# Two-layer hybrid decoder trunk on one core: weight sums in quarter-megabyte pieces, reads moved earlier, stores out of turn, and block attention two rounds deep

## The chip, the cores and the metric

One Trainium2 chip, one of its cores. The metric is the device time of one execution in microseconds (us), the median over several runs. Within a core five engines work beside each other, each on its own list of instructions and in its order: TensorE (PE, matrix products; its weight loads are listed apart as PEld), VectorE (DVE), ScalarE (ACT), GpSimd (POOL) and SyncE (SP, which here only issues DMAs). ACT and POOL issue some DMAs too. An instruction that needs the result of another engine waits at the head of its list, and everything behind it on that engine waits with it.

## The reference, cut to what matters

Two layers over a sequence of 1024 tokens and 1024 channels, float32. One layer:

```python
h = _rms_norm(x, pre_g)
proj = jnp.einsum('bsd,dc->bsc', h, w_in)
sb_qkv, ssm_u, ret_qkv, lru_u, gates, merge = jnp.split(proj, SPLITS, axis=-1)
...
mix = jnp.stack([y_sb, y_ssm, y_ret, y_lru], axis=2).astype(dtype)
mix = mix * jax.nn.silu(gates.reshape(bsz, s, N_BRANCH, BRANCH_WIDTH))
y = jnp.einsum('bsnw,nwd->bsnd', mix, w_branch)
gate = jax.nn.sigmoid(merge.reshape(bsz, s, N_BRANCH, D_MODEL))
merged = jnp.sum(gate * y, axis=2)
out = jnp.einsum('bsd,de->bse', merged, w_out)
return x + _rms_norm(out, post_g)
```

The four mixers are a stick-breaking attention (4 heads of 64, in query blocks of 128), an S5 state space model that ends in GELU and a gated linear unit (GLU), a retention in chunks of 128, and an RG-LRU. The projection `w_in` has 3072 columns for the mixers and their gates (256 for each) and 4096 for the merge gates.

## The kernel before, in words

**Tiling.** Each layer is done in two halves of the sequence, c = 0 and c = 1, of 512 tokens. All large products are of 128x128 weights with 128x512 data in fp32r; float32 accuracy comes from three products (`mm3`, L1200) of a high part `wh` and a low part `wl` of each weight tile with a high and a low part of the data. The gate columns of both halves are multiplied together in a Strassen-like scheme: products of sums of the input (`xs_t`, and the on-chip pieces that hold them, `tab`) with sums of four weight blocks, whose partial results v1, u2, u3 and gate results go to DRAM (`v`, `u`, `ge`) and are fetched back later (`fetch`, L1226).

**The order of the work** is written by hand: the scheduler does not reorder anything. `plan_layer` (L160) lists the fillers of a layer: projections `p` of half 0 with groups `x` of Strassen products between them, projections of half 1, groups `y`, the output product `o` of half 0, groups `z` and merge products `m` of half 1, its output product. Each filler is made of *half fillers*: one weight tile of 128x512 (256 KB), twelve matmuls. There are 268 half fillers in a layer; the number of one is its *position* (p of half 0 and x: 0 to 71, p of half 1: 72 to 103, y: 104 to 179, o: 180 to 195, z and m: 196 to 251, o: 252 to 267).

**What stands ahead of each half filler** is `half(s)` (L1679): `ahead(s)` (L225), where SP issues the reads of weight tiles up to s+9 (`raw`, 8 buffers) and tile s+3 is split (`split`, L111: ACT copies `wh` from `raw`, DVE subtracts to `wl`); `put_late()` (L363), by which SP issues the stores that were asked for at least two positions ago; one function of the list `hooks`; and `planned(l, p)` (L1608), which takes the side generators one step on at the positions that the table `PLAN` gives them: `prep` (parameters, on POOL), `tb` (input of half 1), `lru0/1`, `s50/51` (S5), `ret0/1`, `sb0/1` (attention), `post0/1` (residual and output), `sum` (`wsums`).

**What the change touches.** `wsums(l)` (L1631) makes the sums of the gate weights from DRAM to DRAM: ACT issues copies (`ws<-in_wq_dram`), and POOL issues DMAs that add to them (L1634), each over one piece of 128x2560 floats, 1280 KB. `summed` marks a sum as issued; a weight tile that is a sum (`raw<-ws`) is read after it. `prologue_t(c)` (L392) normalises a half of the input; its squares are made by ACT and added up by POOL (L404). `sba(l, c)` (L1068) is the attention: for each of 16 rounds (4 query blocks by 4 heads) scores on PE against the stored keys `kS` (L106), sigmoids on ACT, a scan and subtraction on DVE (L94), in the next round the transposes of the weights on PE (L1108), and after each second head the product with the values. The queries of a block are read back by SP from DRAM (L1083, `g<-q`); `project` stores them there. `fetch_y` (L1243) fetches what a mixer kept; `gated` (L1232) then multiplies on DVE. `prefetch` (L1270) asks for v1 or u3 one filler ahead, `filler` fetches u2 at its own start. `post` (L1181) adds the residual, which `load_res` reads. `macc` adds merge results on POOL (L1256). All scratch tiles of 128x512 on chip (`G`) come from one pool of NGEN = 50.

```python
# sba, L1078
def queries(b):
    put_late(0)
    S["q", c, b] = (G(F32R), G(F32R))
    for k in range(2):
        assert stored[id(qmem[c][b][k])] == l
        sp.dma_start(S["q", c, b][k].bitcast(F32), qmem[c][b][k])
```

Of the kernel before, what the change touches and what calls it, by code (L numbers as in the profile page):

```python
# [40 lines left out]
def hybrid_kernel(ctx: ExitStack, tc: tile.TileContext, x, xt, ws, wq, wb, par, bcw, preg, postg, con, rot, out, dbg=None):  # L41
# [183 lines left out]
    def ahead(s):  # L225
        load_to(s + NRAW + 1)
        split_to(s + 3)
# [164 lines left out]
    def prologue_t(c):  # L392
        gc = S["par", 0][:, C_PG:C_PG + 8]
        hc = H(F32)
        xk = hc
        for k in range(KD):
            sp.dma_start(xk[k], xt[k, :, c * T:(c + 1) * T])
        yield 0
        acc = G()
        actv(acc, xk[0], AF.Square)  # L400
        for k in range(1, KD):
            sq = G()
            actv(sq, xk[k], AF.Square)
# [12 lines left out]
        yield 0  # L416
        yield from build(hc)
# [650 lines left out]
    def sba(l, c):  # L1068
# [8 lines left out]

        def queries(b):  # L1078
            put_late(0)
            S["q", c, b] = (G(F32R), G(F32R))  # L1080
            for k in range(2):
                assert stored[id(qmem[c][b][k])] == l
                sp.dma_start(S["q", c, b][k].bitcast(F32), qmem[c][b][k])  # L1083

        queries(0)
        for i in range(n + 3):
            yield 3
            if i % 4 == 1 and i < n - 4:
                queries(i // 4 + 1)
            if i >= 2 and i - 2 < n and js[i - 2][1] % 2:  # L1090

                pair = [J.pop(i - 3), J.pop(i - 2)]
# [88 lines left out]
    def post(u):  # L1181
        load_res(u, range(2))
        yield 0
        out_stat(0, NT)
        for t in range(NT):
            yield 0
            out_put(u, t, False)
            load_res(u, range(t + 2, min(t + 3, NT)))
# [37 lines left out]
    def fetch(src, u):  # L1226
        assert stored[id(src)] == u
        t = G()
        sp.dma_start(t, src)
        return t  # L1230
# [12 lines left out]
    def fetch_y(u, n):  # L1243
        l, c = units[u]
        drain(("lru", "s5", "ret", "sb")[n] + str(c))
        put_late(0)
        for j in range(2):
            S["yf", n, j] = fetch(yd[c][n][j], l)
# [20 lines left out]

    def prefetch(l, i):  # L1270

        c, kind, *a = plans[l][i + 1]
        if kind == "y":
            S["v1", a[0]] = fetch(v1d[a[0]], l)
        elif kind == "z":
            for q in a:
                S["u3", q] = fetch(u3d[q], l)

    def filler(l, i, half):
# [66 lines left out]
        elif kind == "z":  # L1346
            m = len(a)
            ps = [A() for _ in range(m)]
            for k in range(2 * m):
                half(s + k)  # L1350
                q, odd = a[k % m], k < m
                if k == 0:
                    for r in a:
                        S["u2", r] = fetch(u2d[r], l)
                        if r % 5 == 0:
                            fetch_y(u, r // 5)
# [21 lines left out]
    def project(u, i, s, half):  # L1378
# [41 lines left out]
        elif i in (9, 11):  # L1420
# [21 lines left out]
            def rest():  # L1442
                for _, _, r_, rd, _ in todo:
                    copy(rd, r_.bitcast(F32))
                if pq:
                    for b in range(NT):
                        for k, t in enumerate(S.pop(("q", b))):
                            store(qmem[c][b][k], t[:, :].bitcast(F32))

            hooks.append(rest)  # L1450
# [180 lines left out]
    def wsums(l):  # L1631
# [3 lines left out]

        for n in ORDER0[l]:
# [22 lines left out]
    with tc.manual_schedule():  # L1659
        dve.memset(ones1, 1.0)  # L1660
        warm = const.tile([P, T], BF16, name="warm")
# [40 lines left out]
NGEN = 50  # L1702
# [13 lines left out]
        "sum": (40, 46, 53, 60, 66, 72, 79, 86, 92, 98, 105, 112, 118, 124, 131, 138, 144, 150, 157, 164, 170),  # L1716
        "sb0": (42, 43, 45, 46, 48, 49, 51, 52, 54, 55, 57, 58, 60, 61, 63, 64, 66, 67, 69, 70, 72, 73, 75, 76, 78, 79, 81, 82, 84, 85, 87, 88, 90, 91, 93, 94, 96, 97, 99, 100),
# [7 lines left out]
    },  # L1725
# [6 lines left out]
        "sum": (30, 37, 44, 51, 58, 65, 72, 79, 86, 93, 100, 107, 114, 121, 128, 135, 142, 149, 156, 163, 170),  # L1732
# [6 lines left out]
    },  # L1739
# [122 lines left out]
```

## Time and profile before

| what | before |
|---|---|
| median of the timed runs (two: 2109.9 and 2103.89) | 2106.89 us |
| the profiled execution, its own time | 2102.62 us |
| its span in the profile | 2100.8 us |
| mean granted clock of TensorE | 0.931 |
| PE busy | 1811.7 us |
| DVE, ACT, POOL busy | 1354.3, 914.5, 408.9 us |
| moved by DMA | 439.52 MB in 213757 packets |

The profile is of one execution. Busy times say how long an engine worked; PE's is the largest. A wait of PE is listed with the engine and line (or the DMA) that ended it. The granted clock is TensorE's: 1.00 is its upper level (2.4 GHz), 0.50 its lower one (1.2 GHz). Line numbers are those of the kernel before.

### The profile page before, as it was taken

The numbers are of one execution on the slowest core, as the hardware profiler recorded it, in microseconds if no ns is written. First come the engines' busy times: TensorE is split into PE (matmuls) and PEld (weight loads), VectorE is DVE, ScalarE is ACT, GpSimd is POOL, SyncE is SP. The second block draws the span as 40 slices with busy tenths as digits, with TensorE's granted clock in tenths as the row PEclk, the third lists the DMA queues.
The fourth block names the chain that finished last, engine by engine and source line by source line (L and its number), as shares of the span: only waits on it lengthen the run. The fifth ranks groups of instructions, "written<-read, shape, count | busy, mean of one in ns | idle before, by whom it ended". The sixth has DMA issues, their size and how long they took to land. (4 is left out here: it accounts for less than half of the span.)

```text
span 2100.8 us, 26957 instructions
## 1 busy us (share of the span) xinstructions
PE 1811.7 (86%) x8730; PEld 1469.7 (70%) x8730; DVE 1354.3 (64%) x2400; ACT 914.5 (44%) x1817; POOL 408.9 (19%) x704
## 2 busy tenths in 40 slices
PE   9576989886997999797899977988799999988997
PEld 6455767764876777676777756767577877766776
DVE  7485466854676774764647875558567767656675
ACT  5465435552332344333455644435433334443333
POOL 6943000000021220586600000000000212100231
PEclk9788999998998999899999988999799999998999
DMA  5259687468888946544526597882889987554543
GB/s 175 84 182 352 203 263 242 126 202 282 231 280 262 296 141 209 195 136 134 163 80 212 182 329 247 262 267 81 239 277 286 299 269 239 179 202 144 169 142 105
DMA packets 213757, 439.52 MB, mean 209 GB/s; under 512 B 25585, under 2 KB 34161, under 8 KB 212593
## 3 DMA queue, kind: packets, MB, share of 16 engines
q1 hardware_dynamic: 203376, 353.92, 49.6%
q0 software_dynamic: 8704, 41.95, 10.6%
q10 hardware_dynamic: 1536, 41.95, 5.4%
q8 instruction: 69, 1.13, 0.2%
q14 instruction: 72, 0.58, 0.1%
HBM read 340.59 MB, written 180.36 MB: 248 GB/s over the span
## 5 line engine op out<-in xcount | busy, mean ns | idle before, releaser
L1207 PE MATMUL pa<-g,wh 128*128 128x512 f32 x2816 | 923.7, 408 | 84.1 <-DVE g L94 46.4
L1207 PEld LDWEIGHTS pa<-g,wh 128*128 128x128 f32 x2816 | 543.3, 197 | 210.1 <-issue 49.0
L94 DVE TENSOR_TENSOR wl<-raw,wh 128x512 fp32r<-128x512 f32 x536 | 408.4, 767 | 347.1 <-ACT wh L91 345.5
L1207 PE MATMUL pa<-g,wl 128*128 128x512 f32 x1368 | 551.1, 403 | 9.2 <-DVE wl L94 9.1
L91 ACT ACTIVATE wh<-raw 128x512 fp32r<-128x512 f32 x536 | 325.3, 626 | 132.5 <-PE pa L1207 64.2
L94 DVE TENSOR_TENSOR g<-g,g 128x512 f32<-128x512 f32 (+7 forms) x427 | 303.6, 719 | 79.8 <-ACT g L91 28.8
L88 ACT ACTIVATE g<-g 128x512 f32<-128x512 f32 (+1 forms) x212 | 132.0, 629 | 488.3 <-DVE g L94 475.1
L1207 PEld LDWEIGHTS pa<-g,wl 128*128 128x128 f32 x1368 | 268.5, 196 | 70.6 <-DVE wl L94 12.0
L94 DVE TENSOR_TENSOR g<-pa,g 128x512 f32<-128x512 f32 x227 | 156.4, 690 | 188.6 <-PE pa L1207 102.5
L1256 POOL TENSOR_TENSOR g<-g,g 128x512 f32<-128x512 f32 x96 | 139.8, 1492 | 512.1 <-DVE g L94 504.3
L1207 PE MATMUL pa<-tab,wh 128*128 128x512 f32 x560 | 187.0, 403 | 12.8 <-DMA tab<-xs_t 12.8
L91 ACT ACTIVATE g<-g 128x512 fp32r<-128x512 f32 (+2 forms) x208 | 112.0, 547 | 173.5 <-DVE g L103 56.2
L1634 POOL DMA_DIRECT2D ws<-in_wq_dram x16 | 14.6, 912 | 698.9 <-DMA ws<-in_wq_dram 698.9
L1207 PE MATMUL pa<-wh,g 128*128 128x512 f32 x448 | 142.2, 399 | 7.3 <-DVE g L94 6.0
L91 ACT ACTIVATE g<-pa 64x128 fp32r<-64x128 f32 (+3 forms) x190 | 92.5, 487 | 109.1 <-PE pa L1207 96.6
L91 ACT ACTIVATE g<-pb 128x128 f32<-128x128 f32 (+5 forms) x227 | 85.5, 421 | 120.2 <-PE pb L106 61.4
L1207 PEld LDWEIGHTS pa<-tab,wh 128*128 128x128 f32 x560 | 107.8, 195 | 36.8 <-DMA tab<-xs_t 11.9
L1207 PE MATMUL pa<-tab,wl 128*128 128x512 f32 x320 | 127.2, 397 | 0.0
L106 PE MATMUL pb<-kS,g 128*128 128x512 f32 (+2 forms) x192 | 57.8, 401 | 57.7 <-DMA g<-q 32.4
L1207 PEld LDWEIGHTS pa<-wh,g 128*128 128x128 f32 x448 | 85.2, 193 | 26.9 <-DVE g L94 6.8
L88 ACT ACTIVATE g<-pb 128x512 f32<-128x512 f32 (+4 forms) x203 | 87.1, 511 | 37.5 <-PE pb L106 22.3
L1207 PE MATMUL pb<-wh,g 128*128 128x512 f32 x320 | 99.3, 392 | 1.0 <-DVE g L94 1.0
(172 smaller groups left out, 1937.1 us busy)
## 6 DMA issues: line engine op xcount, KB each, us to landing
raw<-in_ws_dram SPq DMA_DIRECT2D x192, 256.0 KB, 3.6
ws<-in_wq_dram ACTq DMA_DIRECT2D x32, 1280.0 KB, 9.3
raw<-ws SPq DMA_DIRECT2D x160, 256.0 KB, 4.2
raw<-in_wq_dram SPq DMA_DIRECT2D x120, 256.0 KB, 5.0
ws<-in_wq_dram POOLq DMA_DIRECT2D x16, 1280.0 KB, 11.9
ws<-ws POOLq DMA_DIRECT2D x16, 1280.0 KB, 12.1
u<-g SPq DMA_DIRECT2D x80, 256.0 KB, 5.5
g<-u SPq DMA_DIRECT2D x80, 256.0 KB, 3.5
```

The costliest lines, as they stand in the source:

```text
L88: act.activation(out, in_, func, **kw)
L91: act.activation(out, in_, AF.Copy, **kw)
L94: dve.tensor_tensor(out, a, b, op=op)
L106: pe.matmul(out, lhsT=lhsT, rhs=rhs, start=start, stop=stop)
L1207: pe.matmul(ps, lhsT=a, rhs=b, start=start and i == 0, stop=stop and i == 2, skip_group_check=more)
L1256: pool.tensor_tensor(acc, acc, sg, op=ALU.add)
L1634: pool.dma_start(a, b, accum_op=ALU.add, max_dma_last_dim=5120)
```

## The change

- **Sums by quad.** `wsums` makes each sum in five pieces of 128x512, as the weight tiles are read, each piece with its own copies and additions; ACT issues 160 copies instead of 32 and POOL 160 additions instead of 32. The steps in `PLAN["sum"]` go from 21 to 50 a layer, over positions 38 to 168 (40 to 170 and 30 to 170 before). The old function stays in the file, unused.
- **Reads.** `ahead` asks SP for weight tiles up to s+8 instead of s+9; `split_to` is the same. `prefetch` looks up to four fillers ahead: v1 and u3 up to five half fillers, u2 up to three, and u2 is no longer fetched at the filler's own start. `post` reads one residual piece at a time, ahead of each output step.
- **Stores out of turn.** `stored_now(o)` issues one store early, when something is about to read it; `fetch` and `queries` call it, and `put_late(0)`, which issued all pending stores there, is gone.
- **Query copies** (ACT) and their stores are spread over four hooks, one for each block, instead of one.
- **Attention.** `dp = 2 - c`: in half 0 the transposes of a round come two rounds after its scores instead of one, in half 1 one as before. The queries of the first block are read at position 34 instead of 42 (layer 0), 40 instead of 48 (layer 1) and 106 instead of 116 (half 1); those of the next blocks one round earlier.
- **Input of half 1.** The squares are added up by DVE (`tt`) instead of POOL, seven additions of 128x512.
- **Tables.** The steps of S5 are moved (`s51`: the last ones at 91, 92, 93, 95, 97, 99, 100 instead of 93 to 99; `s50` of layer 0 stretched to 86). The pool has 51 tiles, with the warm-up tile now in it.

```diff
     def ahead(s):
-        load_to(s + NRAW + 1)
+        load_to(s + NRAW)
         split_to(s + 3)
...
+    def stored_now(o):
+
+        for k, e in enumerate(late):
+            if e[0] is o:
+                sp.dma_start(o, e[1])
+                stored[id(o)] = e[3]
+                late.pop(k)
+                return
...
             actv(sq, xk[k], AF.Square)
-            pool.tensor_tensor(acc, acc, sq, op=ALU.add)
+            tt(acc, acc, sq, ALU.add)
...
+        dp = 2 - c
         def queries(b):
-            put_late(0)
             S["q", c, b] = (G(F32R), G(F32R))
             for k in range(2):
+                stored_now(qmem[c][b][k])
...
-        for i in range(n + 3):
+        for i in range(n + dp + 2):
             yield 3
-            if i % 4 == 1 and i < n - 4:
+            if i % 4 == 0 and i < n - 4:
                 queries(i // 4 + 1)
...
-            if 1 <= i <= n:
-                st = J[i - 1]
+            if dp <= i < n + dp:
+                st = J[i - dp]
...
     def prefetch(l, i):
...
+        for k in range(i + 1, min(i + 5, len(plans[l]))):
+            c, kind, *a = plans[l][k]
+            for name, d, reach in (("v1", v1d, 5),) if kind == "y" else (("u3", u3d, 5), ("u2", u2d, 3)) if kind == "z" else ():
+                for q in a if k == i + 1 or base[l, k] - base[l, i] <= reach else ():
+                    if (name, q) not in asked[l]:
+                        asked[l].add((name, q))
+                        S[name, q] = fetch(d[q], l)
...
+            for b in range(NT):
+                hooks.append(lambda b=b: rest(b))
...
+        def cols(a, j):
+            return a[:, 512 * j:512 * j + 512]
+
+        for n in ORDER0[l]:
+            s1, s2, s3, s4 = (wsum[l][j][n] for j in range(4))
+            for j in range(6):
+                if j < 5:
+                    act.dma_start(cols(s3, j), cols(wq[l, n, 2], j))
+                    act.dma_start(cols(s2, j), cols(wq[l, n, 3], j))
+                if j:
+                    add(cols(s3, j - 1), cols(wq[l, n, 0], j - 1))
+                yield 0
+                if j:
+                    add(cols(s2, j - 1), cols(s3, j - 1))
+            summed.update(((l, 1, n), (l, 2, n)))
...
-NGEN = 50
+NGEN = 51
```

**SP, the first query read of layer 0, half 0** (`raw`: weight tiles; `xs`, `xs_t`, `v`: stores of input sums and of Strassen results; `q_0_0`: the queries of block 0). Before, at position 42:

```order
L212 DMA raw_2036<-in_wq_dram 128x512
L366 DMA xs_t_2_304<-g_1983 128x512
L366 DMA xs_t_6_308<-g_1817 128x512
L366 DMA xs_t_2_320<-g_1986 128x512
L366 DMA xs_t_6_324<-g_1919 128x512
L366 DMA xs_t_3_297<-g_2062 128x512
L366 DMA xs_t_7_301<-g_2009 128x512
L1083 DMA g_2071<-q_0_0_262 128x512
L1083 DMA g_2072<-q_0_1_263 128x512
L212 DMA raw_2087<-in_wq_dram 128x512
```

After, at position 34 (L1093 is L1083 of before):

```order
L212 DMA raw_1772<-in_ws_dram 128x512
L366 DMA v_4_150<-g_1710 128x512
L1093 DMA g_1787<-q_0_0_262 128x512
L1093 DMA g_1788<-q_0_1_263 128x512
L212 DMA raw_1805<-in_ws_dram 128x512
L366 DMA v_10_156<-g_1739 128x512
L366 DMA xs_1_287<-g_1755 128x512
```

The read stands eight half fillers earlier, and the six stores that were issued with it at once are no longer ahead of it.

**PE, the second round of that attention** (`kS_94`, `kS_95`: keys of the second and third head; `pa` rows: matmuls of half fillers). Before, with the transpose of the first round (L1108) ahead of the second round's scores:

```order
L1207 MATMUL pa_2129<-g_674,wl_2039 128x512
L1108 MATMUL pb_2220<-cons,g_2104 128x128
L106 MATMUL pb_2224<-kS_94,g_2071 128x256
L106 MATMUL pb_2224<-kS_94,g_2072 128x256
L106 MATMUL pb_2224<-trib,identb 128x128
L1207 MATMUL pa_2130<-g_671,wh_2089 128x512
```

After, the second round:

```order
L1217 MATMUL pa_2137<-g_672,wl_2010 128x512
L106 MATMUL pb_2190<-kS_94,g_1787 128x256
L106 MATMUL pb_2190<-kS_94,g_1788 128x256
L106 MATMUL pb_2190<-trib,identb 128x128
L1217 MATMUL pa_2138<-g_669,wh_2045 128x512
```

And after, the third round (L1118 is L1108 of before; L985 belongs to the retention):

```order
L1217 MATMUL pa_2137<-g_680,wl_2143 128x512
L985 MATMUL pb_2289<-cons,g_1966 128x128 x4
L1118 MATMUL pb_2296<-cons,g_2083 128x128
L106 MATMUL pb_2300<-kS_95,g_1787 128x256
L106 MATMUL pb_2300<-kS_95,g_1788 128x256
L106 MATMUL pb_2300<-trib,identb 128x128
```

The transpose of the first round's weights has moved behind the half fillers between the second and the third round; nothing of the rounds is left out.

**POOL, the sums of layer 0 beside the end of `prep` (L505, L738) and the retention's memsets (L984).** Before:

```order
L738 COPY gp_2049<-gp_893 64x8x16
L984 MEMSET g_2380 128x512
L984 MEMSET g_2381 128x512
L1634 DMA ws_1_0_118<-ws_2_0_122 256x1280
L505 TENSOR_TENSOR gp_893<-cons,par_343 32x128
L505 TENSOR_TENSOR g_2407<-g_2407,gp_893 32x4x32
L505 TENSOR_TENSOR gp_893<-cons,par_343 32x128
L505 TENSOR_TENSOR g_2408<-g_2408,gp_893 32x4x32
L1634 DMA ws_2_2_124<-in_wq_dram 256x1280
```

After (L1646, L747, L993 are L1634, L738, L984 of before):

```order
L1646 DMA ws_1_0_118<-ws_2_0_122 128x512
L1646 DMA ws_2_0_122<-in_wq_dram 128x512
L747 COPY gp_2056<-g_698 64x8x16
L747 COPY gp_2056<-gp_891 64x8x16
L747 COPY gp_2056<-g_698 64x8x16
L747 COPY gp_2056<-gp_891 64x8x16
L1646 DMA ws_1_0_118<-ws_2_0_122 128x512
L1646 DMA ws_2_0_122<-in_wq_dram 128x512
L993 MEMSET g_2392 128x512
L993 MEMSET g_2393 128x512
L1646 DMA ws_1_0_118<-ws_2_0_122 128x512
```

There are more additions, each of a fifth of the bytes, and they stand between POOL's other work, also ahead of the copies and memsets that stood ahead of the sums' second step before.

## Rows read from the trace of the kernel before

**Rows 1.** The page, busy time of each engine.

```profile
PE 1811.7 (86%) x8730; PEld 1469.7 (70%) x8730; DVE 1354.3 (64%) x2400; ACT 914.5 (44%) x1817; POOL 408.9 (19%) x704
```

**Rows 2.** Waits of PE, whole run: us in total, times, longest.

```profile
PE pa L1207 <- DVE g L94: 52.3, 16, 7.5
PE pb L106 <- ACT g L91: 43.8, 13, 11.3
PE pb L1108 <- DVE g L94: 37.5, 16, 6.4
PE pb L106 <- DMA g<-q: 32.4, 4, 18.0
PE pb L106 <- POOL g L404: 21.4, 1, 21.4
```

**Rows 3.** Windows: us, PE, PEld, DVE, ACT, POOL busy, clock, DMA share, GB/s.

```profile
69.70:88.90 19.20, 0.00 (x0) 0.00 (x0) 5.24 (x6) 5.20 (x9) 18.26 (x29) 0.50 0.14 41
91.00:97.00 6.00, 6.00 (x15) 4.65 (x16) 3.47 (x16) 3.36 (x5) 5.05 (x25) 0.50 0.00 0
100.00:106.00 6.00, 6.00 (x28) 4.98 (x27) 5.33 (x17) 3.67 (x10) 5.26 (x19) 1.00 0.00 0
140.00:230.00 90.00, 67.66 (x293) 54.91 (x292) 53.24 (x83) 47.61 (x91) 19.26 (x38) 0.87 1.02 339
178.00:725.00 547.00, 459.73 (x2382) 374.15 (x2380) 345.69 (x634) 211.75 (x418) 57.52 (x74) 0.93 0.79 244
```

**Rows 4.** Groups of instructions, DVE's and POOL's additions: busy, mean ns, idle before.

```profile
L94 DVE TENSOR_TENSOR g<-g,g 128x512 f32<-128x512 f32 (+7 forms) x427 | 303.6, 719 | 79.8 <-ACT g L91 28.8 <-DMA g<-y 27.7 <-ACT g L88 11.2
...
L404 POOL TENSOR_TENSOR g<-g,g 128x512 f32<-128x512 f32 x7 | 9.6, 1372 | 0.4
```

**Rows 5.** Source line of the first query reads, 150 to 200 us.

```profile
L1083 SPq DMA_DIRECT2D g<-q x2: 582/605/628, 194.8 to 195.4; - x2
```

**Rows 6.** Waits of PE by stretch: 262:430, then 1300:1530 (two), 430:512 (two), 825:1000.

```profile
PE pb L1108 <- DVE g L94: 15.4, 6, 6.4
...
PE pb L1108 <- DVE g L94: 15.8, 7, 4.5
PE pb L106 <- ACT g L91: 12.1, 3, 6.1
...
PE pa L1207 <- DMA tab<-xs_t: 12.3, 4, 8.0
PE pb L106 <- ACT g L91: 6.1, 1, 6.1
...
PE pa L1207 <- DVE g L94: 27.1, 7, 7.5
```

**Rows 7.** DMA issues, 628 to 652 us (two), and in the whole run: KB, us to landing.

```profile
ws<-ws POOLq DMA_DIRECT2D x1, 1280.0 KB, 19.2
...
g<-y SPq DMA_DIRECT2D x2, 256.0 KB, 17.2
...
g<-y SPq DMA_DIRECT2D x32, 256.0 KB, 4.5
```

**Rows 8.** Waits of SP, 950 to 975 us.

```profile
SPq L1229 <- POOL g L1256: 18.3, 1, 18.3
```

**Rows 9.** The page, DMA queues: packets, MB, share of 16 engines.

```profile
q1 hardware_dynamic: 203376, 353.92, 49.6%
q0 software_dynamic: 8704, 41.95, 10.6%
q10 hardware_dynamic: 1536, 41.95, 5.4%
```

**Rows 10.** Source lines of the sums: a copy's issue (ACT), an addition's issue (POOL).

```profile
L1638 ACTq DMA_DIRECT2D ws<-in_wq_dram x8: 496/496/604, 178.3 to 1478.5; - x8
...
L1634 POOL DMA_DIRECT2D ws<-in_wq_dram x16: 879/884/1166, 200.3 to 1741.4; - x16
```

More of the change, by code (lines that the diff above doesn't have):

```diff
@@ L1085, in sba @@
         queries(0)
-        for i in range(n + 3):
+        for i in range(n + dp + 2):
             yield 3
-            if i % 4 == 1 and i < n - 4:
+            if i % 4 == 0 and i < n - 4:
                 queries(i // 4 + 1)
-            if i >= 2 and i - 2 < n and js[i - 2][1] % 2:
-                pair = [J.pop(i - 3), J.pop(i - 2)]
+            if 0 <= i - dp - 1 < n and js[i - dp - 1][1] % 2:
+                pair = [J.pop(i - dp - 2), J.pop(i - dp - 1)]
                 b, pq = pair[0]["b"], pair[0]["h"] // 2
@@ L1181, in post @@
     def post(u):
-        load_res(u, range(2))
+        load_res(u, range(1))
         yield 0
@@ L1186, in post @@
             yield 0
+            load_res(u, range(t + 1, min(t + 2, NT)))
             out_put(u, t, False)
-            load_res(u, range(t + 2, min(t + 3, NT)))
     def load_res(u, ts_):
@@ L1226, in fetch @@
     def fetch(src, u):
+        stored_now(src)
         assert stored[id(src)] == u
@@ L1245, in fetch_y @@
         drain(("lru", "s5", "ret", "sb")[n] + str(c))
-        put_late(0)
         for j in range(2):
@@ L1268, in pair @@
             macc(u, n, 2 * i + e, odd if e else S.pop(("ge", 5 * n + 1 + i)), py)
+    asked = [set() for _ in range(DEPTH)]
     def prefetch(l, i):
[L1272 to L1277, printed above, removed]
+        for k in range(i + 1, min(i + 5, len(plans[l]))):
[5 more added lines that the diff above has]
+                        S[name, q] = fetch(d[q], l)
     def filler(l, i, half):
@@ L1353, in filler @@
                     for r in a:
-                        S["u2", r] = fetch(u2d[r], l)
                         if r % 5 == 0:
@@ L1440, in project, with rest @@
                 stt(r_, z, 0.125, q_.bitcast(F32), ALU.mult, ALU.subtract)
-            def rest():
-                for _, _, r_, rd, _ in todo:
+            def rest(b):
+                for _, _, r_, rd, _ in todo[2 * b:2 * b + 2]:
                     copy(rd, r_.bitcast(F32))
                 if pq:
[L1446 to L1450, printed above, removed]
+                    for k, t in enumerate(S.pop(("q", b))):
+                        store(qmem[c][b][k], t[:, :].bitcast(F32))
+            for b in range(NT):
+                hooks.append(lambda b=b: rest(b))
         elif i < 8:
@@ L1634, in add, with wsums_old @@
             pool.dma_start(a, b, accum_op=ALU.add, max_dma_last_dim=5120)
+        def cols(a, j):
[12 more added lines that the diff above has]
+            summed.update(((l, 1, n), (l, 2, n)))
+        for n in range(4):
+            s1, s2, s3, s4 = (wsum[l][j][n] for j in range(4))
+            for j in range(6):
+                if j < 5:
+                    act.dma_start(cols(s1, j), cols(wq[l, n, 2], j))
+                    act.dma_start(cols(s4, j), cols(wq[l, n, 1], j))
+                if j:
+                    add(cols(s1, j - 1), cols(wq[l, n, 3], j - 1))
+                    add(cols(s4, j - 1), cols(s2, j - 1))
+                yield 0
+            summed.update(((l, 0, n), (l, 3, n)))
+    def wsums_old(l):
+        def add(a, b):
+            pool.dma_start(a, b, accum_op=ALU.add, max_dma_last_dim=5120)
         for n in ORDER0[l]:
@@ L1660, in hybrid_kernel @@
         dve.memset(ones1, 1.0)
-        warm = const.tile([P, T], BF16, name="warm")
+        warm = G(BF16)
         dve.memset(warm, 0.0)
@@ L1712 @@
         "lru0": (12, 13, 14, 15, 17, 19, 21, 23, 24, 25, 26),
[1 row of a table removed]
[1 row of a table added]
         "ret0": (46, 48, 51, 53, 55, 58, 60, 62, 65, 67, 69, 72, 74),
         "tb": (14, 15, 16, 17, 19, 20, 21, 22, 23, 24, 26, 27, 28, 29, 30, 31, 33, 34, 35, 36, 37, 38, 40, 41, 42, 43, 44, 45, 47, 48, 49, 50),
-        "sum": (40, 46, 53, 60, 66, 72, 79, 86, 92, 98, 105, 112, 118, 124, 131, 138, 144, 150, 157, 164, 170),
-        "sb0": (42, 43, 45, 46, 48, 49, 51, 52, 54, 55, 57, 58, 60, 61, 63, 64, 66, 67, 69, 70, 72, 73, 75, 76, 78, 79, 81, 82, 84, 85, 87, 88, 90, 91, 93, 94, 96, 97, 99, 100),
[1 row of a table added]
         "pro": (246, 248, 250, 252, 254, 256, 257, 259, 261, 263, 265, 267),
@@ L1720 @@
         "lru1": (78, 80, 82, 83, 85, 87, 89, 91, 92, 94, 96),
[1 row of a table removed]
[1 row of a table added]
         "ret1": (104, 106, 108, 110, 111, 113, 115, 117, 119, 120, 122, 124, 126),
[1 row of a table removed]
[1 row of a table added]
         "post0": (197, 199, 200, 202, 203, 205),
+        "sum": (38, 41, 43, 46, 48, 51, 53, 56, 58, 61, 63, 66, 68, 71, 73, 76, 78, 81, 83, 86, 88, 91, 93, 96, 98, 101, 104, 106, 109, 112, 115, 118, 120, 123, 126, 129, 132, 134, 137, 140, 143, 146, 148, 151, 154, 157, 160, 162, 165, 168),
     },
@@ L1728 @@
         "lru0": (8, 9, 10, 12, 13, 14, 17, 21, 23, 25, 27),
[1 row of a table removed]
[1 row of a table added]
         "ret0": (56, 58, 60, 62, 64, 66, 68, 70, 72, 74, 76, 78, 80),
         "tb": (9, 10, 12, 13, 15, 16, 18, 19, 21, 22, 24, 25, 27, 28, 30, 31, 32, 34, 35, 37, 38, 40, 41, 43, 44, 46, 47, 49, 50, 52, 53, 55, 56),
-        "sum": (30, 37, 44, 51, 58, 65, 72, 79, 86, 93, 100, 107, 114, 121, 128, 135, 142, 149, 156, 163, 170),
[1 row of a table removed]
[1 row of a table added]
         "lru1": (78, 80, 82, 83, 85, 87, 89, 91, 92, 94, 96),
[1 row of a table removed]
[1 row of a table added]
         "ret1": (104, 106, 108, 110, 111, 113, 115, 117, 119, 120, 122, 124, 126),
[1 row of a table removed]
[1 row of a table added]
         "post0": (197, 199, 200, 202, 203, 205),
+        "sum": (38, 41, 43, 46, 48, 51, 53, 56, 58, 61, 63, 66, 68, 71, 73, 76, 78, 81, 83, 86, 88, 91, 93, 96, 98, 101, 104, 106, 109, 112, 115, 118, 120, 123, 126, 129, 132, 134, 137, 140, 143, 146, 148, 151, 154, 157, 160, 162, 165, 168),
     },
```

15 rows, old and new, of the table PLAN are left out of this document.

## Prediction

> **What bounds the kernel now.** I read the busy times first. PE works 1811.7 us of the 2100.8 us span [rows 1], more than any other engine, and the order lists the same matmuls after the change as before; so what can be won is PE's idle time, 289 us, and the time at the lower clock. DVE, at 64%, is second and matters stretch by stretch. Then the waits of PE [rows 2]: no single one rules. Matmuls of half fillers wait for DVE additions 52.3 us in 16 waits, scores for ACT 43.8, transposes (L1108) for DVE's weights 37.5 in 16, scores for the query reads (g<-q) 32.4 in only 4, and one wait for POOL's squares (L404) is 21.4. Then windows [rows 3], which show where these stand: from 140 to 230 us the DMA share is 1.02, so transfers are the bound there, while over 178 to 725 us (half 0 of layer 0, with the sums in it) it is 0.79 and DVE is busy 346 of 547 us. Last, the clock: in the 19.2 us without a matmul it stands at 0.50 and stays there just after it, where 6.0 us hold 15 matmuls, against 28 in 6.0 us at 1.00 [rows 3]. A mean of 0.931 over the span means that 0.069/0.5, 13.8% or 290 us, lie at the lower level. About half of that will be idle time itself; the other half, some 145 us of work, would take 72 less. Per microsecond of idle time that is 72/289 = 0.25. Most waits that go here are short, so I give 0.15 us of clock for each.
>
> **What goes, part by part.** A half filler is twelve matmuls; at 28 in 6.0 us it takes 2.6 us.
>
> (a) Squares on DVE. POOL is busy 18.3 of the 19.2 us in which PE stands, yet its seven additions cost 9.6 us [rows 3, 4]; the rest is parameter work ahead of them in POOL's list. On DVE seven additions cost 7 x 0.719 = 5.0 us [rows 4], beside ACT's squares, and DVE is busy 5.2 of those 19.2 us, so there is room. About 2 us of the wait should stay: 19.4 saved. Bounds: all 21.4 saved, or, if DVE's 5.0 us only push its next work back, 16.4.
>
> (b) Query reads. The 18.0 us wait ends on a read that SP issued at 194.8 us and that landed 4.7 us later [rows 5]: SP was late, not the read slow. In the new order the first read stands eight half fillers earlier, 8 x 2.6 = 21 us of PE work, and six stores no longer stand right ahead of it. That would cover 18.0 if SP were as late as before. But the stretch has a DMA share of 1.02 [rows 3], its bytes are the same, and what is not waited for here may be waited for at the next weight tile. Bounds 0 and 32.4; I take 20 of the 32.4. `load_to` one tile less far ahead moves SP's other DMAs of a half filler forward and no byte; its buffers come free at the same splits: nothing.
>
> (c) Attention two rounds deep. The transposes wait 15.4 us for DVE in half 0 of layer 0 and 15.8 in that of layer 1, 31.2 of the 37.5, the longest 6.4 [rows 2, 6]. The transpose moves one round later, two or three half fillers or 5 to 8 us, behind work that does not need it. So nearly each of these waits is covered: 30. Bounds 0 (if DVE is behind by as much a round later) and 31.2.
>
> (d) Sums in small pieces. At 628 to 652 us the fetch of a mixer's output (g<-y) takes 17.2 us, against 4.5 in the middle over the run, with pieces of 1280 KB in flight [rows 7]; DVE waits 27.7 us for g<-y in all [rows 4], and the longest ACT wait of PE, 11.3, stands behind one of these [rows 2]. Input sums read into tab cost 12.3 in 430 to 512 us [rows 6]. With 256 KB pieces the fetch should be near 4.5, 12.7 less, and the 11.3 go; of the tab waits I take 4.7, since those reads are many. 16 of 23.6; bounds 0 and 23.6.
>
> By the Trainium skill, page "DMA: Bandwidth & Descriptors", section "Queues, rings and completion order", a DMA engine takes its queues in turn, a packet at a time. A big piece then holds up SP's queue by at most a packet and piece size matters less than packet size; here the packets of both kinds shrink, so by it all 23.6 would go, and the sum would be 7.6 better. The 17.2 against 4.5 shows that something holds reads up, but not which of the two.
>
> (e) S5's last steps. PE waits 12.1 in layer 1 and 6.1 in layer 0 for ACT ahead of the GLU [rows 6]; its steps are now spread. I take 12 of 18.2, less 5 for tab reads that these waits hide: 7. Bounds 0 and 18.2.
>
> (f) z fetches. Of the waits for DVE at 825 to 1000 us, 27.1 in 7 [rows 6], some come from operands that arrive late: SP stood 18.3 us there behind POOL's merge addition [rows 8]. Asking up to three half fillers, 7.8 us, earlier for u2 and going past pending stores helps part of it; the rest is DVE's own work. 8; bounds 0 and 27.1.
>
> Idle time gone: 19.4 + 20 + 30 + 16 + 7 + 8 = 100.4. With 0.15 x 100 = 15 for the clock, 115.
>
> **What is added.** ACT issues 128 more copies of 0.496 us each [rows 10], 63.5 us in all over two layers. ACT is busy 212 of 547 us there [rows 3], so most of it lies in idle time; behind such an issue stand the splits and the attention's sigmoids, for which PE waits. Bounds 0 and 63.5; a tenth and a little, 7. POOL issues 128 more additions of 0.884 us, 113 us, and is busy 57.5 of 547 [rows 3, 10]; but an addition that waits for its copy holds up the end of `prep` and the retention's memsets behind it, for which ACT, DVE and SP wait. The waits are shorter than before, since a piece is a fifth. Bounds 0 and 113; I take 5. Spread hooks, the 51st tile, the residual reads: nothing; the next half filler's twelve matmuls hide a 0.5 us copy, and without that cover each would cost its 0.5 us.
>
> Last, what is late next. With PE ahead, the same DVE work (346 of 547 us), splits and reads are asked for sooner. I give back a fifth of 115, 23. Net: 115 - 12 - 23 = 80. The profiled execution took 2102.62 us, its span and 1.8 around it, 4.3 under the median of 2106.89. 2102.6 - 80 = 2023.
>
> **The rivals.**
>
> R1, slower: additions priced by the packet. The POOL queue q0 has 8704 packets in 10.6% of 16 engines' span [rows 9]: 0.106 x 2100.8 x 16 / 8704 = 0.409 us each. These are 272 packets to each of the 32 additions. 160 additions of 128 rows and as many closing packets in the same proportion (144) make 23040. At 0.409 us they take 589 us of the sixteen engines instead of 223, 183 more a layer; 178 to 725 us has 0.79 x 547 = 432 us taken, 615 is 68 over its length. Twice 68 is 136; the gains that don't hang on DMA, (a) and (c) less costs, 38, leave 2200. It decides where the spare 115 us a layer are used up, at 315 ns a packet. Against it: q10 takes 1.18 us for a packet of 27 KB and q1 82 ns for one of 1.74 KB [rows 9]: these two go by bytes, at 23 and 21 KB a us, so for an addition's packet of 2 KB, where one of 4.8 KB takes 409 ns, I expect about half of that.
>
> By the Trainium skill, the same page, section "Anatomy of one DMA", a DMA issued by GpSimd costs about 2.0 us fixed and its bytes at 436 KB a us: an estimate of 2.6 us for 256 KB and 5.0 for 1280 KB, thus 416 us for 160 instead of 160 for 32. That speaks for R1. The trace has 19.2 us for one 1280 KB addition from issue to landing [rows 7], so what it waits for or shares outweighs a fixed 2.0 there.
>
> R2, transfers stay the bound: the bytes of 140 to 230 us are what they were, and waits of (b) and (d) only change their names. 64.4 of idle time and 10 of clock, less 12 and a fifth of 74, 15: 47 saved, 2055. For it: the share of 1.02. Against it: single reads waited 18.0 though they landed in 4.7.
>
> R3, nothing is given back: (a) to (e) go whole, 21.4 + 32.4 + 31.2 + 23.6 + 18.2 = 126.8, and the clock's 19 pay for the added issues and more: 1975. For it: DVE is idle over a third of the time. Against it: the 5 us waits follow DVE's chain itself.
>
> R4, DVE is behind: the transposes of (c) wait as long a round later. 70.4 and 10.6 of clock, less 12 and 16: 53, 2050. For it: the 52.3 us of plain DVE waits. Against it: 346 of 547.
>
> **How the numbers follow.** My forecast .47, R3 .17, R2 .15, R4 .13, R1 .08. 2023 is the likeliest. The range reaches down to R3 with a margin and up past R2 and R4: 1970 to 2075; R1 and a little beside it stay out. A measurement here can tell about 2%, 42 us, from no change, so faster means under 2065 (under 2061 against the profiled execution). The forecast gives .43 faster and .04 same, R3 .17 faster, R2 and R4 (10 and 15 us under that bound) together .165 faster and .115 same, R1 .07 slower and .01 same: .765, .165, .07, rounded below.
>
> **What would show it.** Right: no wait of PE on POOL's squares; g<-q waits under 13 us in all; L1118 waits (the former L1108) under 8 us, all but a few in half 1; g<-y landing near 4.5 us beside the sums; PE's mean clock about 0.95; PE idle about 190 us. A q0 share under 13% of the engines' time is against R1, over 25% for it. Wrong: DMA share at 1.0 through 178 to 725 us; SP or ACT waiting on POOL in layer 0's `prep`; new waits on wh or wl, by which ACT's added issues would cost more than 7 us; a DVE wait in place of each transpose wait.

## The result, and the profile after

The changed kernel took 2032.92 us (two runs, 2029.35 and 2036.49) against 2106.89 before: 74 us less, ratio 0.9649, 95% interval 0.9555 to 0.9743. The forecast was 2023, 80 us less.

The page of the changed kernel, busy times and DMA queues, answers to [rows 1] and [rows 9]:

```profile
PE 1808.2 (89%) x8730; PEld 1464.3 (72%) x8730; DVE 1355.4 (67%) x2407; ACT 917.7 (45%) x1819; POOL 522.2 (26%) x825
...
q1 hardware_dynamic: 203376, 353.92, 51.2%
q0 software_dynamic: 23040, 41.95, 13.1%
q10 hardware_dynamic: 23040, 41.95, 6.0%
```

The span is 2027.6 us, 73.2 less. PE is busy 3.5 us less and idle 219.4 us instead of 289.1, so nearly all of it is idle time. The additions' queue has the 23040 packets that were counted beforehand, at 0.131 x 2027.6 x 16 / 23040 = 184 ns each: well under the 315 ns from which rival R1 would have decided. Its share, 13.1%, is just above the 13% that the forecast named as a sign against R1, and far from the 25% for it.

PE's waits in the changed kernel, whole run (us in total, times, longest), answer to [rows 2]:

```profile
PE pa L1217 <- DVE g L94: 39.2, 15, 7.0
PE pa L1217 <- DMA tab<-xs_t: 23.7, 6, 7.2
PE pb L106 <- DMA g<-ubuf: 22.9, 3, 11.3
PE pb L106 <- ACT g L91: 20.4, 12, 3.9
PE pb L106 <- DVE g L94: 20.3, 11, 4.8
PE pa L1217 <- ACT g L91: 19.3, 4, 7.2
PE pb L1118 <- DVE g L94: 17.3, 9, 3.7
```

The wait for POOL's squares and those for g<-q are gone from the list. The waits for ACT ahead of `pb` matmuls went from 43.8 to 20.4, those of half fillers for DVE from 52.3 to 39.2. Two have grown: reads of S5's input (g<-ubuf) from 1.9 to 22.9, and of Strassen's input sums (tab) from 12.8 to 23.7.

The transposes' total hides two changes. Half 0, now two rounds deep, has none of these waits left. Half 1, one round deep in both kernels, has new ones. First the kernel before from 430 to 1030 us (half 1 of layer 0; in that of layer 1 it has none), then the changed kernel from 430 to 1022 and from 1500 to 2030 us:

```profile
PE pb L1108 <- DVE g L94: 1.9, 1, 1.9
...
PE pb L1118 <- DVE g L94: 8.8, 5, 3.7
...
PE pb L1118 <- DVE g L94: 8.5, 4, 3.6
```

So 35.6 us went in half 0 and 15.4 came up in half 1. The change also moved nearly all steps of half 1's attention (`sb1`) two to four positions forward, and its first ten; no run undoes the former.

The fetches of mixer outputs (g<-y) beside the sums did not come near 4.5 us. Issues of the changed kernel from 585 to 600 us (the place of the 17.2 us of [rows 7]), then from 640 to 656 us:

```profile
g<-y SPq DMA_DIRECT2D x2, 256.0 KB, 6.9
...
g<-y SPq DMA_DIRECT2D x2, 256.0 KB, 14.4
```

The first was 17.2 before; the second is of the next mixer, whose two fetches took 2.9 and 4.5 before. The middle of the eight fetches of that part is 8.1 us, 7.1 before. What did fall is DVE's waits for them, from 27.7 to 6.0 us, none of which is for the 14.4.

One of the forecast's signs of being wrong came up: SP waits for POOL in layer 0's `prep`. POOL's waits from 190 to 222 us, then SP's from 205 to 222 us (L771 copies a table of `prep` for S5; L514 is an addition of `prep`):

```profile
POOL ws L1646 <- DMA ws<-in_wq_dram: 18.4, 3, 7.5
...
SPq L771 <- POOL g L514: 7.1, 1, 7.1
```

POOL stands 18.4 us ahead of additions whose sources have not landed yet, and `prep` stands behind them in its list. Before, SP has no wait for POOL there.

Windows of the changed kernel (us, PE, PEld, DVE, ACT, POOL busy, clock, DMA share, GB/s), answer to the last two of [rows 3]:

```profile
140.00:230.00 90.00, 81.46 (x455) 65.52 (x454) 58.70 (x99) 48.95 (x98) 35.84 (x52) 0.96 1.02 329
178.00:725.00 547.00, 483.89 (x2532) 395.29 (x2532) 368.59 (x665) 228.28 (x450) 117.51 (x134) 0.95 0.85 248
```

From 140 to 230 us PE works 81 us instead of 68, at the same DMA share of 1.02: the transfers are still full there, and PE stands less beside them (the changed kernel is some 20 us further on in its work by then).

Where the gain comes up can be read by the weight tiles: the end of ACT's split number n (`wh<-raw`, counted from 0), of which there are 268 in a layer, set against the changed kernel's (us; worked out from the traces of single executions, whose own spread is some 10 us; the last row is the end of the span).

| n | changed | before | one deep | old S5 steps | paced | later |
|---|---|---|---|---|---|---|
| 32 | 127.7 | +15.8 | -0.7 | -0.5 | +0.2 | -0.7 |
| 64 | 253.5 | +22.8 | -1.5 | -1.8 | -9.9 | -19.6 |
| 128 | 534.7 | +36.7 | +20.2 | +15.5 | -6.3 | -27.8 |
| 160 | 638.1 | +50.8 | +20.2 | +15.5 | -6.3 | -27.5 |
| 256 | 981.8 | +53.7 | +20.5 | +22.5 | -6.3 | -20.0 |
| 400 | 1556.9 | +74.2 | +28.1 | +39.0 | -12.0 | -56.9 |
| 536 | 2027.6 | +73.2 | +22.1 | +34.6 | -18.6 | -51.2 |

Before, 37 of the 73 us were lost by n = 128, 14 more between 128 and 160, and 20 in half 0 of layer 1. The other columns are experiments below.

### The profile page after: what moved, and what is told of

Same layout as the page of the kernel before. It is cut to its first block, busy times and chain, and to the rows that moved or that the text cites. A ratio compares the mean times of both kernels' runs of the same rounds, so it can differ in the third digit from the quotient of the medians.

```text
span 2027.6 us, 27353 instructions
## 1 busy us (share of the span) xinstructions
PE 1808.2 (89%) x8730; PEld 1464.3 (72%) x8730; DVE 1355.4 (67%) x2407; ACT 917.7 (45%) x1819; POOL 522.2 (26%) x825
## 3 DMA queue, kind: packets, MB, share of 16 engines
q1 hardware_dynamic: 203376, 353.92, 51.2%
q0 software_dynamic: 23040, 41.95, 13.1%
q10 hardware_dynamic: 23040, 41.95, 6.0%
## 5 line engine op out<-in xcount | busy, mean ns | idle before, releaser
L1217 PE MATMUL pa<-g,wh 128*128 128x512 f32 x2816 | 918.3, 405 | 65.3 <-DVE g L94 30.6
L94 DVE TENSOR_TENSOR wl<-raw,wh 128x512 fp32r<-128x512 f32 x536 | 404.3, 760 | 351.4 <-ACT wh L91 332.5
L94 DVE TENSOR_TENSOR g<-g,g 128x512 f32<-128x512 f32 (+7 forms) x434 | 313.1, 730 | 41.6 <-ACT g L91 16.1
L1646 POOL DMA_DIRECT2D ws<-in_wq_dram x80 | 72.0, 900 | 629.4 <-DMA ws<-in_wq_dram 596.3
L1217 PE MATMUL pa<-tab,wh 128*128 128x512 f32 x560 | 190.3, 409 | 23.7 <-DMA tab<-xs_t 23.7
L1646 POOL DMA_DIRECT2D ws<-ws x80 | 70.0, 875 | 265.1 <-DMA ws<-in_wq_dram 186.3
L88 ACT ACTIVATE g<-pb 128x512 f32<-128x512 f32 (+4 forms) x203 | 87.2, 511 | 31.2 <-PE pb L106 19.4
```

The lines of the kernel that those rows point to most:

```text
L88: act.activation(out, in_, func, **kw)
L94: dve.tensor_tensor(out, a, b, op=op)
L1217: pe.matmul(ps, lhsT=a, rhs=b, start=start and i == 0, stop=stop and i == 2, skip_group_check=more)
L1646: pool.dma_start(a, b, accum_op=ALU.add, max_dma_last_dim=5120)
```

## The experiments

All are built on the changed kernel. Its own time is 2033 (2032.92, and 2034.45 in a second series of four runs, 2028.92 to 2038.43). The other medians are of four runs, which lie 2 to 20 us apart, so a difference under some 6 us is not told apart.

**The same kernel again.** No edit.

> The changed kernel once more, as the measure for the others of this series on the same chip. Every theory: 2033 us, within 5.

2034.45, ratio to before 0.9635 (0.9596 to 0.9675).

**Squares on POOL.**

```diff
-            tt(acc, acc, sq, ALU.add)
+            pool.tensor_tensor(acc, acc, sq, op=ALU.add)
```

> The changed kernel with the seven additions of squares of half 1's input on POOL again. By the forecast: the wait of PE at about 67 us comes back with some 20 us, +22 with the clock: about 2055 us. By the rival that what follows (the build of half 1's input on DVE, 12.9 us of wait before, 7.2 now) decides when that stretch ends: +10 us or less, or, if the stretch gets longer by DVE's late start too, +27.

2047.33, ratio 0.9709 (0.9676 to 0.9742): 13 us slower. The waits of PE from 60 to 135 us, squares on POOL:

```profile
PE pb L106 <- POOL g L413: 21.5, 1, 21.5
PE pa L1217 <- ACT g L91: 9.5, 1, 9.5
```

The wait is back whole, and the next one, for half 1's input, is 9.5 where the changed kernel has 7.2 and the kernel before 12.9. Of these some 20 us, 13 reach the end. The forecast's mechanism holds, its size less a third.

**Attention one round deep.**

```diff
-        dp = 2 - c
+        dp = 1
```

with the old steps of `sb0` after the first.

> The changed kernel with the attention of half 0 one round deep again (transposes a round after the scores, the old steps), the first queries still read early. By the forecast: the transposes wait some 30 us more in half 0, +35 with the clock, less a fifth, +28: about 2061 us. By the rival that DVE is behind anyway and two rounds only move the wait: under +10 us.

2051.79, ratio 0.9727 (0.9692 to 0.9763): 18 us slower. First line of PE's waits, whole run, one round deep:

```profile
PE pb L1118 <- DVE g L94: 64.2, 26, 12.6
```

The transposes wait 47 us more than in the changed kernel, all of it in half 0. Yet only 18 us come out at the end: in the table the loss begins between n = 64 and 128, is 20 in layer 0 and hardly grows in layer 1. The rival's "under 10" falls; the forecast's 28 was too much. Other waits are shorter here: g<-ubuf fell from 22.9 to 12.2.

**First queries late.**

```diff
-        "sb0": (34, 42, 43, 45,
...
+        "sb0": (42, 42, 43, 45,
...
-        "sb1": (106, 116, 119,
...
+        "sb1": (116, 116, 119,
...
```

(and 40 to 48 in layer 1).

> The changed kernel with the first queries of each half read at the old positions (42, 48, 116). By the forecast most of (b) hangs on the lead of eight half fillers: PE waits for g<-q again, some 15 to 20 us over the run, +15 to +20 us: about 2050. By the rival that SP's order (no pending stores ahead of the read, tiles a half filler less ahead) did it: g<-q waits under 8 us and under +6 us.

2031.71, ratio 0.9616 (0.9578 to 0.9655): no change that can be told. Neither theory was right. The waits came back:

```profile
PE pb L106 <- DMA g<-q: 23.9, 2, 13.9
```

Where the time went is seen in two windows, first of this kernel, then of the changed one:

```profile
140.00:180.00 40.00, 26.04 (x107) 20.88 (x107) 29.03 (x44) 21.36 (x39) 15.83 (x26) 0.79 1.05 364
220.00:260.00 40.00, 40.00 (x247) 34.20 (x246) 19.08 (x31) 14.13 (x31) 4.95 (x6) 1.00 0.93 252
```

```profile
140.00:180.00 40.00, 35.82 (x164) 28.77 (x163) 30.82 (x47) 25.27 (x47) 11.70 (x16) 1.00 1.03 370
220.00:260.00 40.00, 33.21 (x189) 28.40 (x188) 15.65 (x26) 11.66 (x26) 6.61 (x9) 0.91 0.88 229
```

PE stands 10 us more early on and 7 less later (and 4 less between the two): the DMA engines are full in the first window either way, and after the wait the reads behind it have landed; the changed kernel's wait of 6.8 us for g<-ubuf at 244 us isn't there. The other wait, 10.0 us in layer 1, stands in a stretch of the same kind: from 1180 to 1260 us the DMA share is 0.99 in both kernels, and PE works 65.3 us here, 64.7 in the changed one. This is rival R2, for the lead of the queries.

**Sums in big pieces, with their old steps.**

```diff
-"sum": lambda l: wsums(l)
+"sum": lambda l: wsums_old(l)
```

> The changed kernel with the sums in pieces of 1280 KB again and the old steps for them; all else as changed. By the forecast's terms the small pieces save 18 us (16 of waits, 2 of clock) and cost 12 in issues, so undoing them gives +6: about 2039 us, with g<-y fetches beside the sums at 15 us or more again and PE's tab<-xs_t waits over the 23.7 us of the changed kernel. By the rival that the transfers are the bound there: within 3 us of 2033, with waits under other names. By a second rival, that the pieces carry most of the gain: +25 us or more.

2026.6, ratio 0.9603 (0.9573 to 0.9633): if anything 8 us faster, on no side of what was expected. In the trace it is 16 us ahead by n = 80, 11 to 14 through the rest of layer 0, and loses that in layer 1. Of the signs, one fetch of a mixer's output took 18 us (in layer 1), but the tab waits are 20.5, not more. So the small pieces either cost something in themselves or are issued at the wrong time.

**Small pieces, paced as of old.** Only the numbers of `PLAN["sum"]`: 50 steps evenly from 40 (30 in layer 1) to 170.

> The changed kernel with its small pieces, but their 50 steps spread evenly over the old stretch (40 to 170 in layer 0, 30 to 170 in layer 1) instead of crowded into the first half. If the crowding cost the 12 to 16 us that the kernel with big sums was ahead by in half 0 of layer 0: about 2020 us, and PE reaches the y fillers of layer 0 about 10 us earlier. If the number of pieces costs it (128 more issues on ACT and on POOL, packets of 2 KB): within 4 us of the changed kernel of this series.

2008.9, ratio 0.9516 (0.9485 to 0.9547): 25 us faster than the changed kernel, with the same 320 issues. So it is not the number of pieces that costs but when they come: the numbers of one table. What in them decides is not told by this run. "Crowded", as the expectation has it, is too strong: the first 24 steps take 60 positions in the changed kernel and 64 here; in layer 0 they come 2 to 6 positions later, in layer 1 up to 8 earlier. Over the same stretch of positions small pieces beat big ones by 2026.6 - 2008.9 = 18 us.

**Small pieces, later.** Steps at 56 to 140 for the sums that y needs, 143 to 195 for the rest.

> The changed kernel with its small pieces begun later and spread further: the sums that y needs at positions 56 to 140, the others at 143 to 195, in both layers. If the crowding of transfers in half 0 is what the small pieces cost (the kernel with them paced as of old stood at 2009, the changed one at 2034), leaving the most crowded stretch altogether gives more: about 2000 us, with most of it by the 64th half filler of each layer. If the pace of the first steps only mattered by ACT's and POOL's issues beside prep and attention, or the sums now collide with y and z: 2009 or more, with waits on wl, wh or g<-y in y and z.

1976.36, ratio 0.9383 (0.9355 to 0.9412): 57 us faster than the changed kernel, more than expected, and the fastest here: it beats both. In the table 20 us of it come by n = 64 and 28 by n = 128, 8 of which are lost again by n = 256, and 37 in half 0 of layer 1. Windows of this kernel, then of the changed one:

```profile
180.00:220.00 40.00, 39.51 (x278) 32.35 (x277) 23.03 (x47) 19.71 (x44) 10.81 (x21) 1.00 0.75 238
220.00:260.00 40.00, 40.00 (x233) 33.82 (x233) 24.25 (x45) 15.85 (x35) 4.67 (x6) 1.00 0.86 236
...
520.00:750.00 230.00, 219.35 (x1097) 180.10 (x1096) 150.19 (x218) 93.62 (x191) 75.08 (x74) 0.99 0.95 276
```

```profile
180.00:220.00 40.00, 35.64 (x235) 28.17 (x236) 22.88 (x44) 19.49 (x43) 20.83 (x33) 0.91 1.04 323
...
520.00:750.00 230.00, 218.12 (x1103) 179.67 (x1104) 163.65 (x255) 92.50 (x190) 59.13 (x53) 0.99 0.78 232
```

From 180 to 260 us PE stands half a microsecond in all, with the DMA share at 0.75 and 0.86; in the changed kernel it stands 4.4 of the first 40 us, at 1.04, and 6.8 of the next (its row is with the late queries above). And from 520 to 750 us the share rises from 0.78 to 0.95 at no cost there: PE works 219 and 218 of 230 us. POOL's waits for the sums' sources from 180 to 215 us and SP's for `prep` are gone too. So two things have left that stretch, bytes and POOL's waits; this run doesn't tell them apart, nor the later start from the later end.

**Big pieces, later.** 21 steps spread evenly from 56 to 195.

> The changed kernel with pieces of 1280 KB on the later steps (21 steps from 56 to 195, in both layers). Small pieces on these steps stood at 1976 us, big ones on the old steps at 2027. If size and time are independent, small pieces being worth 18 us at equal steps (2009 against 2027): about 1994 us, with waits behind a big piece (wl, g<-xs_t, g<-y, tab) in layer 1 that the small ones don't have. If only the time at which the bytes move matters: within 6 us of 1976. If big pieces now collide with y and z: 2010 or more.

2001.57, ratio 0.95 (0.9468 to 0.9532). Small pieces are worth 25 us at these steps and 18 at the old ones; the later steps are worth 25 us with big pieces (2026.6 to 2001.57) and 33 with small (2008.9 to 1976.36). Size and time are two gains that add up, as far as 7 us tell (the small pieces' steps are denser towards the end of the stretch than the even ones here). PE's waits with big pieces on later steps (whole run):

```profile
PE pb L106 <- DMA g<-ubuf: 29.8, 4, 11.6
PE pa L1217 <- DMA tab<-xs_t: 29.3, 7, 10.3
...
PE pa L1217 <- DMA g<-xs_t: 15.8, 2, 8.3
```

75 us of waits for SP's reads; with small pieces on these steps g<-ubuf is 8.0, tab 28.4, and g<-xs_t not among the fifteen longest.

**Old reads and stores.** `load_to` a tile further, `put_late(0)` ahead of queries and mixer fetches, `prefetch` one filler ahead, u2 at its filler.

> The changed kernel with the old rules for reads and stores (tiles up to s+9, all pending stores ahead of a query read or a mixer fetch, v1 and u3 one filler ahead, u2 at its own filler); the attention, its early first queries, sums and tables as changed. By the forecast, which put 8 us on the z fetches, 10 of the 20 us of the query reads on the order of SP, and some of the y wait on it: +15 to +20 us, with most of it at z (positions 196 to 251) and at the first queries. By the rival that SP's order decides nothing while transfers are the bound: within 4 us.

2044.12, ratio 0.9685 (0.9653 to 0.9717): 10 us slower, half of what the forecast would have, and not where it put it: 8 of the 18 us by which its trace is behind are lost by n = 112, and at z, where the forecast had 8, none are. DVE's waits for mixer outputs come back (27.7 before). They go with the order of reads and stores, not with the size of the pieces: changed kernel, then big sums, then old reads:

```profile
DVE g L94 <- DMA g<-y: 6.0, 4, 2.7
...
DVE g L94 <- DMA g<-y: 4.2, 3, 3.4
...
DVE g L94 <- DMA g<-y: 20.3, 10, 4.7
```

**Both: big sums and old reads.**

> The changed kernel with both the big sums (and their old steps) and the old rules for reads and stores. Alone the first took 8 us off and the second put 10 on. If they are independent: about 2036 us. If each alone suffices to cure the wait for a mixer's output in the y fillers (11.3 us before, in neither of the two kernels with one of them undone), that wait comes back here: some 12 to 15 us more, about 2050, lost between the 128th and the 160th half filler, with a g<-y fetch of 15 us or more.

2062.45, ratio 0.9797 (0.9758 to 0.9837): 28 us slower, where the two alone sum to 2. In the trace 13 us fall between n = 144 and 160; where the rest of the difference comes up isn't placed. PE's waits there (590 to 640 us), then the DMA issues of that stretch (KB, us to landing):

```profile
PE pb L1118 <- DVE g L94: 12.0, 1, 12.0
```

```profile
ws<-in_wq_dram ACTq DMA_DIRECT2D x2, 1280.0 KB, 13.3
...
g<-y SPq DMA_DIRECT2D x2, 256.0 KB, 15.4
```

The fetch of a mixer's output is slow beside big pieces again, as in [rows 7]. With either cure alone that wait isn't there: the fetch took 8.7 us with big sums and new reads, 4.1 with small sums and old reads. Undoing one part alone shows none of this gain. A slow fetch alone doesn't make the wait: for the 14.4 us of the changed kernel DVE doesn't wait.

**Old steps of S5.** The rows `s50` and `s51` of `PLAN` as before.

> The changed kernel with the old steps of S5 in both halves. By the forecast's terms the moved steps are worth 7 us (12 of GLU waits less 5 of tab reads): about 2040 us, with some 15 us of waits for ACT and DVE ahead of the GLU again. By the rival that they give as much back, since S5's end of half 0 and its start of half 1 now meet in SP's list (g<-ubuf waits of 23 us): 2033 or less, with g<-ubuf waits under 8 us.

2055.16, ratio 0.975 (0.9724 to 0.9776): 21 us slower, three times the forecast's 7. PE's waits with the old steps, from 310 to 430 us, then in the changed kernel:

```profile
PE pb L106 <- ACT g L91: 14.2, 3, 9.3
PE pb L106 <- DVE g L94: 9.0, 4, 6.7
```

```profile
PE pb L106 <- DMA g<-ubuf: 11.3, 1, 11.3
PE pb L106 <- DVE g L94: 1.5, 2, 0.9
```

The rival was half right: the new steps do trade the GLU's waits for one on g<-ubuf (SP stores S5's input and reads it back, and here the end of half 0's S5 does the same in between). But it is 23.2 us of waits against 12.8, in this stretch alone. The longest, 9.3, is at the GLU of half 0 (n = 79), where the kernel before, with the same steps, waits 0.7.

**S5's stores first.**

```diff
         for h in range(2):
-            regroup(vp[h], U[h], ubuf[h], True)
+            sp.dma_start(ubuf[h], vp[h][:, :])
+        for h in range(2):
...
```

> The changed kernel with one thing turned round in S5: both halves of its input are stored to DRAM first and then both are read back, so that SP stands once for a store to land and not twice. In the changed kernel PE waits 22.9 us for these reads (g<-ubuf), 1.9 before. By the theory that this is a new wait that gave back part of the gain: 8 to 15 us less than the changed kernel, with g<-ubuf waits under 10 us. By the rival that the time is bound by what comes behind (DVE's scans, transfers): within 4 us, the wait only changes its name.

2024.2, but its runs spread from 2020.82 to 2040.52, ratio 0.9608 (0.956 to 0.9656): not told apart. The g<-ubuf waits did not fall, 26.4. The theory that SP's second wait for a landing makes them falls. What makes them stays open: they are 8.0 with small sums on later steps and 29.8 with big ones there, but 8.8 with big sums on the old steps and 12.9 with small ones.

## Why the prediction was right, and where it was not

The size, 74 against 80, is right. Of its marks, the g<-q waits (none), the waits on squares (none) and the clock (0.945) came out as written. PE's idle time is 219 us, not 190; the transposes' waits are 17.3, not 8; the g<-y fetches beside the sums are not near 4.5 us (the middle over the whole run, 4.4, was 4.5 before too); and SP's wait for POOL, 7.1 us, was a sign of being wrong. Several terms were off, and cancel, so that the closeness is in part luck. By undoing each part (medians against 2034; the forecast's terms with their 0.15 of clock, before the fifth given back):

| part | forecast | undone: slower by |
|---|---|---|
| (a) squares | 22 | 13 |
| (b) lead of the queries | 23, with SP's order | -2 |
| (c) two rounds deep | 35 | 18 |
| (d) small sums | 18 less 12 of costs | -8 |
| (e) S5's steps | 8 | 21 |
| (b, f) reads and stores | 9, and a share of (b) | 10 |
| (d) with reads and stores | | 28 |

13 + 18 + 21 + 28 - 2 = 78 accounts for the 74, within what five such differences can say. That the last row is 26 more than its two parts is why undoing parts one by one finds only 52. The spread query copies, the residual reads, the 51st tile and the moved steps of half 1's attention were undone in no run.

(a) and (c) were right in kind: no wait on POOL's squares, no wait of transposes in the attention of half 0. But "19.4 saved" and "nearly each of these waits is covered: 30" were taken as time at the end, and it was a third to a half less: what one wait loses, others win back. The fifth that was given back belonged here, and was larger. (c) also read half 1 wrongly: it put 31.2 of the 37.5 us in half 0, where 35.6 stood, 4.4 of them ahead of the window that it read, and it did not foresee the 15.4 that came up in half 1.

(b) failed at "I take 20 of the 32.4". The waits for g<-q went whole, which the forecast had as a mark of being right, and were worth nothing: the DMA share of 1.02, which the forecast weighed and let take off a third, decided. In both stretches tried here, with DMA shares of 0.99 to 1.05, such a wait was worth what the transfers let PE do, not its own length.

(d) failed in its reason and in what was added. "The fetch should be near 4.5" did not come out (6.9 and 14.4 beside the sums), though the wait of 11.3 us behind it went. DVE's waits for these fetches went by the new order of reads and stores, whatever the size of the pieces (6.0 and 4.2 us with it, 20.3 and 17.7 without). The size of the pieces was worth 18 to 25 us, as the term said (18), by whatever way. The cost named was 12 us of ACT's and POOL's issues, 5 of them for additions that hold up the end of `prep`, and the new steps of the table were taken as neutral. But against other steps with the same issues the changed ones cost 25 us, and 57 against those that leave positions 38 to 55, where the transfers are full, and go on to 195. POOL's 18.4 us at the end of `prep` are a candidate for a part of it in layer 0; no run moves them alone. Why the even steps, so near to the changed ones, win as much as they do, above all in layer 1, stays open.

By the Trainium skill, page "DMA: Bandwidth & Descriptors", section "Queues, rings and completion order", a DMA engine takes its queues in turn, a packet at a time, and a packet there is some 9 to 17 descriptors. The prediction took it for the packets that the trace counts (144 to a piece of 256 KB, 272 to one of 1280 KB) and worked out 7.6 us more; no run shows that the two are the same. The 18 to 25 us measured for the size fit the 18 taken and that figure alike.

(e) was a mis-sized term: 7 without the clock, measured 21. The GLU waits of the kernel before were counted, but not the DVE waits beside them, nor the 9.3 us that the old steps cost at half 0's GLU once the other parts are in place; and 5 us were taken off for tab reads. Of the 12.1 us that it read in layer 1, 10.4 stand at the GLU. The tab waits did grow (12.8 to 23.7 over the run), and the g<-ubuf waits as well (1.9 to 22.9), which the forecast didn't name. (f) put 8 us at z; with the old reads nothing was lost there.

R1 is out, at 184 ns a packet (its 38 for (a) and (c) less costs is 37.4; nothing hangs on it). By the Trainium skill, the same page, section "Anatomy of one DMA", each such DMA costs about 2.0 us fixed beside its bytes. Here one of 256 KB takes 7.0 us to land in the middle, where one of 1280 KB took 12.1, both beside other transfers: a line through the two leaves 5.7 us at no bytes (an estimate from these two). It is latency, though: the queue's share of the engines rose from 10.6% to 13.1% only. R3 and R4 are out as they were put: much was given back, and half 0's transposes did not wait a round later. R2 holds for the query reads, and fits the time of the sums; the gains of (c), (e) and the small pieces stand beside it.

The clock gave less than the 15 us of the sum: PE is busy 3.5 us less. That can't be set apart from the spread: the changed kernel's second profile has PE busy 1813.9 us.

## What to carry to other kernels

Where the DMA engines are full, a wait may have no price of its own: look at the window's DMA share first, and try moving transfers out of the full stretch before moving instructions in it. Background transfers have a size and a time, and both have to be chosen: here the small pieces were worth some 20 us, and the steps that came with them took that back, while steps in the emptier part of the layer gave 57 over the changed kernel. Here POOL stood until each one's source had landed, so look at what else is in the list of the engine that issues them. Judge a transfer by its landings in the stretch that matters: the middle over the run did not move here. Undo parts in pairs as well as one by one, since two cures for one wait hide each other.

## What the runs showed of the hardware that was not expected

An addition's packet of about 1.8 KB (41.95 MB over 23040) takes 184 ns where one of 4.8 KB took 409, and a copy's 0.060 x 2027.6 x 16 / 23040 = 84 ns where one of 27 KB took 1.18 us: cutting packets to a fifteenth cost the copies little, 6.0% of the engines' time for 5.4%.

PE's busy time for the same 8730 matmuls ran from 1789.9 us (big pieces, later) to 1826.6 us (old S5 steps) at mean granted clocks of 0.950 and 0.933. It does not follow the idle time: the former stands 210 us and the latter 236, but the changed kernel, with 219, has 1808.2. Where matmuls of equal work differ by up to 37 us, small gains need several runs.
